# A planner's model of PSUM turns and of two operation costs, and the places of the keys' transfers and of the convolution's weights

## The chip, the cores and the metric

The kernel runs on one core of a Trainium2 chip. The metric is the device time of one execution in microseconds (us), smaller is better; a time given for a kernel is the median of several executions. Profiled executions carry a trace of every instruction, and their span is the time from the first to the last of them.

Engines are named as the profile names them: PE multiplies matrices, DVE and ACT work on vectors, POOL does small side work, and SP issues every transfer (DMA).

## What is computed

Two layers of a decoder trunk on 512 tokens of width 1024. Each layer projects its input to four branches, gates each branch, projects it back, merges the four and normalises. Cut to what matters here:

```python
for l in range(2):
    h = x @ W_in                      # one projection, its columns shared out to the branches
    ya = rwkv7(...)                   # 8 heads x 64: decay, delta-rule state over time
    yb = latent_attention(...)        # 8 heads, low-rank q and kv, one rotary key for all heads, causal
    yc = conv_module(...)             # glu -> causal depthwise conv, width 31 -> LayerNorm -> swish
    ym = cross_attention(x, mem, ...) # 4 heads x 128 over 256 memory tokens
    out = merge(gate(ya), gate(yb), gate(yc), gate(ym)) @ W_out
    x = LayerNorm(alpha * x + out)
```

Everything is float32. A product is made as three passes over a high and a low part of each factor (high by high, high by low, low by high), so each weight block of 128x1024 is loaded, rounded to its high part by ACT (names like `w11h`) and its rest taken by DVE (`w11l`).

## The kernel before

The program is written by a planner. `Plan` (L69) keeps a clock for PE, ACT, DVE and POOL, the time at which each tile was last written (`done`), and a queue of tasks, which are Python generators. Each task says up to which time it must wait, and the planner always lets the task run whose time is due by PE's clock; when none is due, the main stream goes on. What a task issues is put on the engines at that place and stays in that order, so the planner's guess of the times fixes the order on every engine, and the chip's semaphores then add the true waits. The guess has these parts:

- `Plan.start` (L91): an operation starts when its engine is free and each tile it reads or writes is done, plus a latency for the way from one engine to the other. Tiles that are only read hold nobody up.
- `Engine.__getattr__` (L210): the cost of an operation from its size. An ACT operation costs 65 + 0.83 ns per column, with more for a scale or a bias in a tile; the sum that it may leave beside (`accum_out`) costs nothing. A DVE reciprocal falls under the rule for all others, 65 + 1.04 ns per column.
- `Space` (L243): PSUM tiles, taken and given back; a tile that takes over a slot waits for the last use of the one before. The tags "ps" and "pp" are the PSUM tiles that the tasks share.

**Weights.** The main stream is a list of items; an item names the weight blocks that it needs, the work that it does with them, and a condition for being picked. The stream picks the next item whose condition holds, and asks for its weights ahead: up to four blocks (`LOOK`), through two raw buffers (`WR`) and three pairs of split buffers (`WH`). Every transfer stands in one queue, on SP, in program order, so a transfer that waits for its data holds up all behind it.

**The convolution** has four pairs of items (`conv_items`): glu0 to glu3 give the gate, val0 to val3 the value, each a projection of 24 passes. val of a pair may be picked when `L["glus"]` is above its number; this counter goes up when the gate's activation is issued, behind its 24 passes.

**The rotary key** (`key_rotary`): one 32x512 key for all heads is split into `krh` and `krl`, and these are copied by eight transfers into the eight tiles `kT` (four pairs, high and low), 2 us of the planner's time between pairs, starting when the split is done.

**RWKV units** (`rwkv_unit`): two units of four heads per half, eight in all (two layers). In each unit PE fills the tile `y0` (named `x_..x` in the trace): its left half is read by DVE into `BP` (two multiplies), its right half by ACT into `RA` (two copies), in this order, by the task `others`. After it, `w` is PE's small product of the running state `S`, and `QQ`, `PP` are DVE's steps of the next inverse.

**The softmax of the latent attention** runs per block of queries: PE makes scores `ms`, DVE masks them and takes the maximum (`nmm`), ACT takes the exponential with its row sum (`mP`, `smm`), DVE takes the reciprocal and scales, PE transposes `mP` into `mt`, ACT copies it (`mPT`), and PE makes `mo`. `xs`, `xP`, `xt`, `xo` are the same steps of cross-attention.

Nearly all instructions come from four helper lines: L237 (DVE, ACT, POOL), L288 (matmul), L293 (transpose) and L300 (transfer), so they are told apart by tile names.

Of the kernel before, what the change touches and what calls it, by code (L numbers as in the profile page):

```python
# [62 lines left out]
CH_P, CH_RG, CH_MG, CH_U, CH_CG, CH_XQ, CH_XG, CH_M = 0, 13, 17, 21, 29, 33, 37, 41  # L63
# [3 lines left out]
class Plan:  # L67
# [13 lines left out]
    def __init__(self, keep):  # L81
        self.keep = keep
        self.clk = {"PE": 0.0, "ACT": 0.0, "DVE": 0.0, "POOL": 0.0}
        self.t = self.queue = self.wires = 0.0
        self.cut, self.cuts = (128, 128), 0
        self.tasks = []
        self.done = {}
        self.seen = {}
        self.slots = {}

    def start(self, eng, outs, ins):  # L91
        s = self.clk.get(eng, 0.0)
        for n in outs + ins:
            t, e = self.done.get(n, (0.0, eng))
            s = max(s, t + self.lat(e, eng))
        return s

    def end(self, eng, t, outs, ins):
        for n in outs:
            self.done[n] = (t, eng)  # L100
        for n in outs + ins:
            self.seen[n] = max(t, self.seen.get(n, 0.0))

    def op(self, eng, cost, outs, ins):
        t = self.start(eng, outs, ins) + cost
        self.clk[eng] = t
        self.end(eng, t, outs, ins)
        self.t = max(self.t, t)
# [92 lines left out]
def _names(*aps):  # L201
    return [a.tensor.name for a in aps if hasattr(a, "tensor")]


class Engine:
# [5 lines left out]
    def __getattr__(self, name):  # L211
        f = getattr(self.eng, name)

        def call(*a, **k):
            o = k.get("out", a[0] if a else None)
            i = k.get("in_", k.get("in0", a[1] if len(a) > 1 else o))
            n = 1
            for d in (o if name in ("activation", "copy") or self.key == "POOL" else i).shape[1:]:
                n *= d
            if self.key == "ACT":  # L220
                c = 65 + 0.83 * n + 120 * hasattr(k.get("scale"), "tensor") + 90 * hasattr(k.get("bias"), "tensor")
            elif self.key == "POOL":
                c = 200 + 167 * n if k.get("op") == ALU.pow else 250 + 1.6 * n
            elif name == "tensor_tensor_scan":
                c = 65 + 2.1 * n
            elif name == "scalar_tensor_tensor":
                c = 128 + 1.04 * n if hasattr(k["scalar"], "tensor") else 75 + 1.03 * n
            elif name == "tensor_scalar" and hasattr(k["scalar1"], "tensor"):
                c = 152 + 1.12 * n if hasattr(k["scalar2"], "tensor") else 134 + 0.52 * n
            elif name in ("tensor_scalar", "tensor_copy"):  # L230
                c = 70 + 0.85 * n
            else:
                c = 65 + 1.04 * n
            args = list(a) + list(k.values())
            outs = _names(o, k.get("accum_out"))
            self.plan.op(self.key, c, outs, [x for x in _names(*args) if x not in outs])
            return self.plan.keep(f(*a, **k))  # L237

        return call


class Space:
# [18 lines left out]
    def tile(self, shape, dt, tag, name, bufs=None):  # L261
        t = self.pool.tile(shape, dt, tag=tag, name=name, **({} if bufs is None else {"bufs": bufs}))
        self.plan.slot((id(self.pool), tag), bufs or self.bufs, t.tensor.name)
        return t


@with_exitstack
def trunk_kernel(ctx: ExitStack, tc: tile.TileContext, A, out, dbg=None):
    nc = tc.nc
    plan = Plan(tc.keep_in_program_order)  # L270
    V, S, G = Engine(plan, nc.vector, "DVE"), Engine(plan, nc.scalar, "ACT"), Engine(plan, nc.gpsimd, "POOL")
# [30 lines left out]
    def pool(bufs, **k):  # L302
        return Space(plan, ctx.enter_context(tc.tile_pool(bufs=bufs, **k)), bufs)
# [7 lines left out]
    pp = pool(2, name="pp", space=PSUM)  # L311
# [29 lines left out]
    def cc(n):  # L341
        return cst[:, CCOL[n][0]:CCOL[n][1]]
# [297 lines left out]
    def layer_items(l):  # L640
        items = []
        L = {}
# [12 lines left out]
        def item(blocks, run, ready=None, picked=None, soon=None):  # L655
            items.append((blocks, run, ready, picked, soon))

        def ch_item(i, name, after, ready=None, picked=None):

            def run(get):  # L660
                ps = yield from project(get, X[l], name + t_)
                after(ps)
                yield
            item([(A["w_ch"][l, i], (512, 512))], run, ready, picked)
# [92 lines left out]
        SUB = range(2)  # L757
# [5 lines left out]
        def by2(ap):  # L763
            return ap.rearrange("p (a b) w -> p a b w", a=2)
# [5 lines left out]
        def rwkv_unit(j0, hf, rkv):  # L770
            t = f"_{l}_{j0}_{hf}"
# [8 lines left out]
            def rk(tag, shape, name=None, dt=F32, bufs=1):  # L780
                return L["rp"].tile([128] + shape, dt, tag=tag, name=(name or tag) + t, bufs=bufs)
# [27 lines left out]
            bt, kt, w = rk("bt", [2, 256]), rk("kt", [2, 256]), rk("s4", [2, 256], "w")  # L809
# [16 lines left out]
            for s in SUB:  # L826
                for cp, c2, h in quads:
                    c = 2 * cp + c2
                    MM(g0[HALF[c2], h, 128 * s + 64 * cp:128 * s + 64 * cp + 64], bt[HALF[h], s, 64 * c:64 * c + 64], AR[HALF[h], s, c, 0], start=True, stop=True, four=True)
            for s in SUB:  # L830
                for cp, c2, h in quads:
                    c = 2 * cp + c2
                    MM(g0[HALF[c2], h, 256 + 2 * s + cp:257 + 2 * s + cp], sq[HALF[h], s, 64 * c:64 * c + 64], bones2[HALF[h], h:h + 1], start=True, stop=True, four=True)
            gvs = [g1[:, :, 256 * s:256 * s + 256].rearrange("p h (a w) -> p h a w", a=2) for s in SUB]
            for s in SUB:
                for cp, c2, h in quads:
                    c = 2 * cp + c2
# [131 lines left out]
            x0, y0 = yield from pg.take([128, 2, 512], "x0" + t, 2, soon)  # L969
            x0, y0 = (x.rearrange("p c (q s a w) -> p q s c a w", q=2, s=2, a=2) for x in (x0, y0))  # L970
# [5 lines left out]
            for s in SUB:  # L976
                for cp, c2, h in quads:
                    c = 2 * cp + c2
# [10 lines left out]
            def others():  # L989

                yield
                for s in SUB:
                    V.tensor_tensor(out=by2(BP[s])[:, :, :, 64:128], in0=y0[:, 0, s],
                                    in1=cc("minc").unsqueeze(1).unsqueeze(1).to_broadcast([128, 2, 2, 64]), op=ALU.mult)
                for s in SUB:
                    S.copy(by2(RA[s])[:, :, :, 64:128], y0[:, 1, s].rearrange("p h c w -> p c h w"))
                pg.free()
                vt.extend((yield from tokens(2, vr, lambda: place("bt", "vt"))))

            vt = []  # L1000
            RA = [rk(f"s{4 + s}", [4, 128], f"RA{s}") for s in SUB]
# [53 lines left out]
            gb, hh, y0 = ([x[:, :, a:b].rearrange("p c (a w) -> p c a w", a=2) for x in gbs] for a, b in ((0, 256), (256, 384), (384, 512)))  # L1055
            for s in SUB:
                for cp, c2, h in quads:
                    MM(gb[s][HALF[h], c2, cp], VA[s][HALF[c2], 2 * (h ^ cp) + cp, 64:128], BP[s][HALF[c2], 2 * h + cp], start=True, stop=True, four=True)
                for cp in range(2):
                    for first in (True, False):  # L1060
                        for c2 in range(2):
                            for h in range(2):
                                e = 2 * h + cp
                                x, y = (bk1[s][:, e], vt[s][:, e]) if first else (BP[s][:, e, 0:64], VA[s][:, 2 * (h ^ cp) + cp, 0:64])
                                MM(hh[s][HALF[h], c2, cp], x[HALF[c2]], y[HALF[c2]], start=first, stop=not first, four=True)
                for h in range(2):
                    for first in (True, False):
                        for cp in range(2):
                            for c2 in range(2):
                                e = 2 * h + cp  # L1070
# [20 lines left out]
            for c in range(4):  # L1091
                e = 2 * (c % 2) + c // 2
                if hf == 0 and c == 0:
                    states.append([H[:, s, 0] for s in SUB])
                elif hf == 0 or c < 3:
                    ps, = yield from pa.take([128, 2, 64], f"w{c}" + t, 1, "pe" if diag else "small")
# [18 lines left out]
            ps, = yield from pg.take([128, 2, 512], "yb" + t, 1, soon)  # L1115
# [33 lines left out]
            ps, = yield from pa.take([128, 512], "ty" + t)  # L1149
# [101 lines left out]
        def conv_items(i):  # L1251
            d = {}

            def glu(ps):
                d["t"] = sp.tile([128, 512], F32, tag="tg", bufs=3, name=f"tglu{i}" + t_)
                S.activation(d["t"], ps, AF.Tanh, scale=0.5)
                L["glus"] += 1

            def val(ps):
                hpad = hpads[i % 2]  # L1260
                V.scalar_tensor_tensor(out=hpad[:, 30:542], in0=d["t"], scalar=1.0, in1=ps, op0=ALU.add, op1=ALU.mult)
                plan.spawn(taps(i, hpad))
                L["vals"] += 1

            ch_item(CH_U + 4 + i, f"glu{i}", glu, lambda: L["vals"] >= i - l and (i < 2 or L["taps"][i - 2] >= 20))
            ch_item(CH_U + i, f"val{i}", val, lambda: PRM[l] is not None and L["glus"] > i and (i < 2 or L["taps"][i - 2] == 30))


# [120 lines left out]
        def key_rotary():  # L1389

            kpe, ts = L["kpe"], u("rk" + t_, 256)
            k4 = kpe.rearrange("p (a d) -> p a d", a=4)
            yield lambda: angles
            rope(k4[:, :, 0:16], k4[:, :, 16:32], [ts[:, 64 * i:64 * i + 64].rearrange("p (a d) -> p a d", a=4) for i in range(4)], lambda f: f)
            ps, = yield from pa.take([128, 512], "kr" + t_)
            plan.due(kpe)
            yield "pe"
            for tb in range(4):
                TR(ps[0:32, 128 * tb:128 * tb + 128], kpe[:, 32 * tb:32 * tb + 32])
            yield  # L1400
            kr = [u(f"kr{n}" + t_, 512, F32R, 32) for n in "hl"]
            yield from split(*kr, ps[0:32])
            pa.free()
            plan.due(*kr)
            yield
            for kT in L["kT"]:
                for x, y in zip(kT, kr):
                    DMA(x[64:96].bitcast(F32), y.bitcast(F32))
                plan.t += 2000.0
                yield  # L1410
# [725 lines left out]
```

## Time and profile before

| what | value |
|---|---|
| time, median of 3 runs | 1481.37 us (1480.49 to 1482.63) |
| the profiled execution's own time | 1482.08 us |
| its span | 1480.3 us |
| granted PE clock, mean | 0.998 of full speed |
| PE busy | 1465.0 us, 99% of the span |
| DVE busy | 1037.4 us, 70% |
| ACT busy | 682.5 us, 46% |
| POOL busy | 145.2 us, 10% |

The rows of a timeline give an instruction's start in us, its length, engine, line, operation and tiles (output<-input); "x4" means a run of four like it, and a bracket tells how long the engine had been idle before it and what ended that. PE's passes overlap: the record of a pass lasts longer than the distance to the next one, so a gap between records is shorter than the time by which a pass started late.

### The profile page before, as it was taken

What the parts mean: (1) busy time and instruction counts of PE and PEld (TensorE: products, weight loads), DVE (VectorE), ACT (ScalarE), POOL (GpSimd) and SP (SyncE); (2) the same over time, 40 slices, a digit from 0 to 9 for tenths busy, and PEclk for the clock granted to TensorE, in tenths of its full rate; (3) what the DMA queues carried; (4) which work ended last, traced back from release to release, by engine and by line L of the source; (5) the groups of instructions that cost most, each with busy time, mean ns of one, the idle gap of its engine ahead of it and who ended that gap; (6) DMA issues with size and microseconds to landing.
All of it is one profiled execution on the core that took longest, in us unless ns stands there. A gap on an engine that the chain in (4) does not pass through costs nothing.

```text
span 1480.3 us, 28872 instructions
## 1 busy us (share of the span) xinstructions
PE 1465.0 (99%) x11727; PEld 1232.7 (83%) x11727; DVE 1037.4 (70%) x2022; ACT 682.5 (46%) x1327; POOL 145.2 (10%) x337
## 2 busy tenths in 40 slices
PE   9999999999999999999999999999999999999997
PEld 8888888888888888888999888888888788888886
DVE  6799998765757666545564889987856476756757
ACT  5546653425354544343264466633454454444331
POOL 0000000030303030000010000000041103121002
PEclk9999999999999999999999999999999999999999
DMA  6444332223232223333353252423232313233532
GB/s 216 139 127 110 86 115 93 93 75 97 68 89 74 84 75 103 122 117 130 113 165 109 74 148 74 121 92 104 81 95 76 95 51 106 71 101 113 172 94 78
DMA packets 89157, 153.49 MB, mean 104 GB/s; under 512 B 41024, under 2 KB 47424, under 8 KB 89024
## 3 DMA queue, kind: packets, MB, share of 16 engines
q1 hardware_dynamic: 89024, 151.65, 34.2%
q8 instruction: 92, 1.51, 0.4%
q14 instruction: 41, 0.34, 0.1%
HBM read 134.32 MB, written 5.77 MB: 95 GB/s over the span
## 4 chain that ended last, share of the span: by engine, by line
PE 89%; DVE 4%; DMA 3%; ACT 2%; POOL 1%; issue 1%; SPq 0%; ACTq 0%; DVEq 0%; POOLq 0%
PE ps_m L288 24%; PE po L288 12%; PE ps_cg L288 3%; PE ps_rg L288 3%; PE ps_xg L288 3%; PE ps_mg L288 3%; PE ps_xq L288 3%; PE ps_val L288 3%; PE ps_v L288 3%; PE ps_r L288 2%; PE pz L288 2%; PE ps_k L288 2%; PE ps_glu L288 2%; PE ms L288 2%; PE x L288 2%; DMA w<-in_w_ch_dram 1%
## 5 line engine op out<-in xcount | busy, mean ns | idle before, releaser
L237 DVE SCALAR_TENSOR_TENSOR cacc<-hpad,prm,cacc 128x512 f32<-128x512 f32 x240 | 179.1, 748 | 4.0
L237 ACT ACTIVATE tm<-ps_m,prm 128x512 f32<-128x512 f32 x64 | 44.1, 689 | 164.3 <-PE ps_m L288 163.6
L237 DVE SCALAR_TENSOR_TENSOR mt<-tm,po 128x512 f32<-128x512 f32 x48 | 33.0, 687 | 88.7 <-PE po L288 88.6
L237 POOL TENSOR_TENSOR tmpW<-ZT,W 64x14 f32<-64x14 f32 (+6 forms) x112 | 43.8, 391 | 8.0
L237 POOL TENSOR_SCALAR ZT<-W 64x256 f32<-64x256 f32 x8 | 5.8, 728 | 369.5 <-DMA W<-scr 144.6
L237 ACT ACTIVATE mP<-ms,nmm 128x128 f32<-128x128 f32 (+3 forms) x64 | 33.8, 530 | 17.6 <-DVE nmm L237 11.5
L237 POOL TENSOR_TENSOR ZT<-ZT,tmpW 64x14 f32<-64x14 f32 (+6 forms) x112 | 39.6, 354 | 8.8
L237 DVE TENSOR_TENSOR merged<-merged,mt 128x512 f32<-128x512 f32 x48 | 33.7, 702 | 1.7
L237 ACT COPY mPT<-mt 128x128 f32<-128x128 f32 (+3 forms) x64 | 26.1, 429 | 17.0 <-PE mt L293 16.6
L237 POOL MEMSET D<- 128x8 f32 x8 | 0.9, 112 | 327.0 <-PE ms L288 310.3
L237 DVE CUSTOM_DVE_ANT_0 ms<-ms,causal 128x128 f32<-128x128 f32 (+3 forms) x64 | 31.0, 499 | 0.2
L237 POOL TENSOR_SCALAR lrs<-lmv 128x1 f32<-128x1 f32 x8 | 4.0, 503 | 244.2 <-DVE lmv L237 239.3
L293 PE MATMUL mt<-cst,mP 128*128 128x128 f32 x160 | 26.3, 273 | 1.5 <-DVE smx L237 1.0
L237 DVE TENSOR_SCALAR mP<-mP,smm 128x128 f32<-128x128 f32 (+3 forms) x64 | 24.8, 387 | 2.4
L237 DVE SCALAR_TENSOR_TENSOR merged<-tm,po 128x512 f32<-128x512 f32 x16 | 11.0, 687 | 21.6 <-PE po L288 21.6
L293 PEld LDWEIGHTS mt<-cst,mP 128*128 128x128 f32 x160 | 19.6, 140 | 7.2 <-ACT xP L237 1.4
L237 ACT ACTIVATE yb<-yb,mr,gr 128x64 f32<-128x64 f32 x64 | 22.1, 428 | 2.9 <-DVE mr L237 2.9
L237 ACT ACTIVATE xP<-xs,nmx 128x256 f32<-128x256 f32 x32 | 15.2, 475 | 13.2 <-DVE nmx L237 11.4
L288 PE MATMUL ms<-kTl,qT 96*128 96x128 f32 (+3 forms) x64 | 21.1, 329 | 0.0
L237 ACT ACTIVATE z<-z,lnb,lrs 128x256 f32<-128x256 f32 (+2 forms) x11 | 7.0, 666 | 30.2 <-DVE lnb L237 30.2
L288 PE MATMUL ms<-kTh,qT 96*128 96x128 f32 (+3 forms) x64 | 20.6, 322 | 0.0
L288 PE MATMUL ms<-kTh,qTl 96*128 96x128 f32 (+3 forms) x64 | 20.6, 322 | 0.0
(3575 smaller groups left out, 5220.4 us busy)
## 6 DMA issues: line engine op xcount, KB each, us to landing
w<-in_w_ch_dram SPq DMA_DIRECT2D x146, 512.0 KB, 3.6
w<-in_w_o_dram SPq DMA_DIRECT2D x32, 512.0 KB, 3.6
w<-in_w_out_dram SPq DMA_DIRECT2D x16, 512.0 KB, 3.5
w<-in_w_lat_dram SPq DMA_DIRECT2D x15, 336.0 KB, 3.0
w<-in_w_mk_dram SPq DMA_DIRECT2D x8, 512.0 KB, 3.5
w<-in_w_mv_dram SPq DMA_DIRECT2D x8, 512.0 KB, 3.7
w<-in_w_qk_dram SPq DMA_DIRECT2D x8, 320.0 KB, 3.0
x<-in_xT_dram SPq DMA_DIRECT2D x8, 256.0 KB, 5.0
```

The costliest lines, as they stand in the source:

```text
L237: return self.plan.keep(f(*a, **k))
L288: plan.keep(nc.tensor.matmul(o, lhsT, rhs, start=start, stop=stop))
L293: plan.keep(nc.tensor.transpose(o, i, ident))
```

## The change

There are five edits, all in what the planner believes or in when a task asks for something. No operation of the computation is added or left out.

- **Turns.** PSUM tiles with the tags "ps" and "pp" now carry a note of who last read them and when. In the plan, an engine that reads such a tile starts no earlier than 130 ns after another engine's read has ended.
- **Costs.** An ACT operation that leaves a sum costs 130 ns more, and a DVE reciprocal costs 90 + 4 ns per column.
- **RA or BP first.** In `others`, ACT's copies into `RA` are issued ahead of DVE's multiplies into `BP` when ACT's clock stands behind DVE's.
- **Convolution weights.** In layer 0, `L["glus"]` goes up when glu is picked (`first`), not when its activation is issued, so val0's weights can be asked for right behind glu0's. In layer 1 it goes up as before.
- **Keys' transfers.** `key_rotary` waits 4 us of the planner's time before its first transfer.

```diff
@@ -87,12 +87,16 @@
         self.done = {}
         self.seen = {}
         self.slots = {}
+        self.read = {}
 
     def start(self, eng, outs, ins):
         s = self.clk.get(eng, 0.0)
         for n in outs + ins:
             t, e = self.done.get(n, (0.0, eng))
             s = max(s, t + self.lat(e, eng))
+        for n in ins:
+            t, e = self.read.get(n, (0.0, eng))
+            s = max(s, t + (130.0 if e != eng else 0.0))
         return s
 
     def end(self, eng, t, outs, ins):
@@ -100,6 +104,9 @@
             self.done[n] = (t, eng)
         for n in outs + ins:
             self.seen[n] = max(t, self.seen.get(n, 0.0))
+        for n in ins:
+            if n in self.read:
+                self.read[n] = t, eng
 
     def op(self, eng, cost, outs, ins):
         t = self.start(eng, outs, ins) + cost
@@ -218,9 +225,11 @@
             for d in (o if name in ("activation", "copy") or self.key == "POOL" else i).shape[1:]:
                 n *= d
             if self.key == "ACT":
-                c = 65 + 0.83 * n + 120 * hasattr(k.get("scale"), "tensor") + 90 * hasattr(k.get("bias"), "tensor")
+                c = 65 + 0.83 * n + 120 * hasattr(k.get("scale"), "tensor") + 90 * hasattr(k.get("bias"), "tensor") + 130 * ("accum_out" in k)
             elif self.key == "POOL":
                 c = 200 + 167 * n if k.get("op") == ALU.pow else 250 + 1.6 * n
+            elif name == "reciprocal":
+                c = 90 + 4 * n
             elif name == "tensor_tensor_scan":
                 c = 65 + 2.1 * n
             elif name == "scalar_tensor_tensor":
@@ -261,6 +270,8 @@
     def tile(self, shape, dt, tag, name, bufs=None):
         t = self.pool.tile(shape, dt, tag=tag, name=name, **({} if bufs is None else {"bufs": bufs}))
         self.plan.slot((id(self.pool), tag), bufs or self.bufs, t.tensor.name)
+        if tag in ("ps", "pp"):
+            self.plan.read[t.tensor.name] = 0.0, ""
         return t
 
 
@@ -989,11 +1000,19 @@
             def others():
 
                 yield
+
+                def right():
+                    for s in SUB:
+                        S.copy(by2(RA[s])[:, :, :, 64:128], y0[:, 1, s].rearrange("p h c w -> p c h w"))
+
+                first = plan.clk["ACT"] < plan.clk["DVE"]
+                if first:
+                    right()
                 for s in SUB:
                     V.tensor_tensor(out=by2(BP[s])[:, :, :, 64:128], in0=y0[:, 0, s],
                                     in1=cc("minc").unsqueeze(1).unsqueeze(1).to_broadcast([128, 2, 2, 64]), op=ALU.mult)
-                for s in SUB:
-                    S.copy(by2(RA[s])[:, :, :, 64:128], y0[:, 1, s].rearrange("p h c w -> p c h w"))
+                if not first:
+                    right()
                 pg.free()
                 vt.extend((yield from tokens(2, vr, lambda: place("bt", "vt"))))
 
@@ -1254,7 +1273,7 @@
             def glu(ps):
                 d["t"] = sp.tile([128, 512], F32, tag="tg", bufs=3, name=f"tglu{i}" + t_)
                 S.activation(d["t"], ps, AF.Tanh, scale=0.5)
-                L["glus"] += 1
+                L["glus"] += l
 
             def val(ps):
                 hpad = hpads[i % 2]
@@ -1262,7 +1281,11 @@
                 plan.spawn(taps(i, hpad))
                 L["vals"] += 1
 
-            ch_item(CH_U + 4 + i, f"glu{i}", glu, lambda: L["vals"] >= i - l and (i < 2 or L["taps"][i - 2] >= 20))
+            def first():
+                if l == 0:
+                    L["glus"] += 1
+
+            ch_item(CH_U + 4 + i, f"glu{i}", glu, lambda: L["vals"] >= i - l and (i < 2 or L["taps"][i - 2] >= 20), first)
             ch_item(CH_U + i, f"val{i}", val, lambda: PRM[l] is not None and L["glus"] > i and (i < 2 or L["taps"][i - 2] == 30))
 
 
@@ -1402,6 +1425,7 @@
             yield from split(*kr, ps[0:32])
             pa.free()
             plan.due(*kr)
+            plan.t += 4000.0
             yield
             for kT in L["kT"]:
                 for x, y in zip(kT, kr):
```

Since the order follows from the plan, it moves in many places. Three of them are shown; numbers behind a name are buffer numbers, and a bracket lists the queues whose semaphores a row waits for.

**SP, at the start of layer 0.** The rows are transfers; `in_w_ch` holds the projection's blocks, `in_w_mk` those of the memory's keys, `krh` and `krl` are the split rotary key. Before:

```order
L300 DMA w_464<-in_w_ch_dram 128x1024
L300 DMA w_494<-in_w_mk_dram 128x1024
L300 DMA w_537<-in_w_mk_dram 128x1024
L300 DMA kTh_0_356<-krh_580 32x512
L300 DMA kTl_0_357<-krl_581 32x512
L300 DMA w_609<-in_w_ch_dram 128x1024
L300 DMA kTh_0_358<-krh_580 32x512
L300 DMA kTl_0_359<-krl_581 32x512
L300 DMA kTh_0_360<-krh_580 32x512
L300 DMA kTl_0_361<-krl_581 32x512
L300 DMA w_648<-in_w_mk_dram 128x1024
L300 DMA kTh_0_362<-krh_580 32x512
```

After:

```order
L311 DMA w_464<-in_w_ch_dram 128x1024
L311 DMA w_494<-in_w_ch_dram 128x1024
L311 DMA w_537<-in_w_mk_dram 128x1024
L311 DMA w_603<-in_w_mk_dram 128x1024
L311 DMA kTh_0_356<-krh_583 32x512
L311 DMA kTl_0_357<-krl_584 32x512
L311 DMA w_649<-in_w_ch_dram 128x1024
L311 DMA kTh_0_358<-krh_583 32x512
L311 DMA kTl_0_359<-krl_584 32x512
L311 DMA kTh_0_360<-krh_583 32x512
L311 DMA kTl_0_361<-krl_584 32x512
L311 DMA w_699<-in_w_ch_dram 128x1024
```

val0's block, `w_609` before and `w_494` now, moves from behind the keys' first pair to the place right behind glu0's block (`w_464`); the two blocks of memory keys stay ahead of the pair, and what stands behind the pair now is the block of glu1, `w_649`.

**ACT and DVE, second unit of layer 1** (`x_1_0_1x` is its `y0`; `w194h` and `w194l` are the split of a weight block; `cb` is a PSUM tile of the convolution's output, which `yc` reads). ACT before, with its waits:

```order
L237 COPY PT_0_1_12808<-x_1_0_1_12734 128x4x64 x2
L237 COPY RA_1_0_1_12813<-x_1_0_1x 128x4x64 [waits DVE_49,PE_49]
L237 COPY RA_1_0_1_12814<-x_1_0_1x 128x4x64
L237 CAST w194h<-w_12878 128x1024 [waits DMAHW6_49,PE_49,Activation_49]
L237 ACTIVATE yc_1_12897<-cb_1_12880,prm_7759 128x512 [waits PE_49]
```

ACT after:

```order
L246 COPY PT_0_1_12808<-x_1_0_1_12734 128x4x64 x2
L246 COPY RA_1_0_1_12813<-x_1_0_1x 128x4x64 [waits PE_49]
L246 COPY RA_1_0_1_12814<-x_1_0_1x 128x4x64
L246 CAST w194h<-w_12878 128x1024 [waits DMAHW6_49,PE_49,Activation_49]
L246 ACTIVATE yc_1_12897<-cb_1_12880,prm_7759 128x512 [waits PE_49]
```

DVE before:

```order
L237 SCALAR_TENSOR_TENSOR mt_1_12824<-tm_1_12689,po_1_12724 128x512 [waits DVE_49,PE_49]
L237 TENSOR_TENSOR merged_1_10994<-merged_1_10994,mt_1_12824 128x512 [waits DVE_49]
L237 TENSOR_TENSOR BP_1_0_1_12510<-x_1_0_1x,cst 128x4x64
L237 TENSOR_TENSOR BP_1_0_1_12511<-x_1_0_1x,cst 128x4x64
L237 SCALAR_TENSOR_TENSOR S_1_0_0_12870<-w_1_0_0_12833,dl_0_0_11387,H_0_0_12216 128x64 [waits PE_49]
```

DVE after:

```order
L246 SCALAR_TENSOR_TENSOR mt_1_12824<-tm_1_12689,po_1_12724 128x512 [waits DVE_49,PE_49]
L246 TENSOR_TENSOR merged_1_10990<-merged_1_10990,mt_1_12824 128x512 [waits DVE_49]
L246 TENSOR_TENSOR BP_1_0_1_12510<-x_1_0_1x,cst 128x4x64 [waits Activation_49]
L246 TENSOR_TENSOR BP_1_0_1_12511<-x_1_0_1x,cst 128x4x64
L246 SCALAR_TENSOR_TENSOR S_1_0_0_12870<-w_1_0_0_12833,dl_0_0_11384,H_0_0_12216 128x64 [waits PE_49]
```

The rows keep their places; the wait between the two readers of `y0` changes sides. Of the eight units, ACT's `RA` waits for DVE in all eight before and in two after; in the other six DVE's `BP` waits for ACT.

**PE, softmax of layer 0** (the block whose transposed probabilities are made from `mP_0_1538` before and `mP_0_1539` after; their scores are `ms_0_1521` and `ms_0_1524`, a few rows earlier). Before:

```order
L288 MATMUL ms_0_1543<-kTl_0_363,qT_0_1208 128x128 [waits DMAHW6_49,DMAHW4_49,Activation_49]
L288 MATMUL ms_0_1543<-kTh_0_362,qT_0_1208 128x128 [waits DMAHW2_49]
L288 MATMUL ms_0_1543<-kTh_0_362,qTl_0_1209 128x128 [waits DMAHW0_49]
L293 MATMUL xt_0_1531<-cst,xP_0_1317 128x128 x2
L293 MATMUL xt_0_1531<-cst,xP_0_1421 128x128 x2
L293 MATMUL mt_0_1565<-cst,mP_0_1499 128x128 [waits DVE_49,Activation_49]
L293 MATMUL mt_0_1565<-cst,mP_0_1499 128x128 x3
L293 MATMUL mt_0_1573<-cst,mP_0_1538 128x128 [waits DVE_49,Activation_49]
L288 MATMUL ms_0_1575<-kTl_0_361,qT_0_1206 128x256 [waits Activation_49]
L288 MATMUL ms_0_1575<-kTh_0_360,qT_0_1206 128x256
L288 MATMUL ms_0_1575<-kTh_0_360,qTl_0_1207 128x256
```

After:

```order
L304 MATMUL mt_0_1557<-cst,mP_0_1501 128x128 [waits DVE_49,Activation_49]
L304 MATMUL mt_0_1557<-cst,mP_0_1501 128x128 x3
L299 MATMUL ms_0_1565<-kTl_0_361,qT_0_1206 128x256 [waits Activation_49]
L299 MATMUL ms_0_1565<-kTh_0_360,qT_0_1206 128x256
L299 MATMUL ms_0_1565<-kTh_0_360,qTl_0_1207 128x256
L304 MATMUL xt_0_1544<-cst,xP_0_1317 128x128 x2
L304 MATMUL xt_0_1544<-cst,xP_0_1424 128x128 x2
L299 MATMUL mo_0_1247<-mPT_0_1395,v_0_928 64x128 [waits Activation_49]
...
L299 MATMUL mo_0_1247<-mPT_0_1519,v_0_931 64x128
L304 MATMUL mt_0_1602<-cst,mP_0_1539 128x128 [waits DVE_49,PE_49]
L304 MATMUL mt_0_1610<-cst,mP_0_1552 128x128 [waits DVE_49,Activation_49]
```

The single transpose of that block stood behind four transposes of the block before; now three score passes, four transposes `xt` and the product `mo` stand between them.

## The prediction

> **What bounds the kernel now.** I read the page's busy shares and its chain first, then the busy time by stretches, then the list of what PE waited for, and last the timeline at each of those waits.
>
> ```profile
> PE 1465.0 (99%) x11727; PEld 1232.7 (83%) x11727; DVE 1037.4 (70%) x2022; ACT 682.5 (46%) x1327; POOL 145.2 (10%) x337
> PE 89%; DVE 4%; DMA 3%; ACT 2%; POOL 1%; issue 1%; SPq 0%; ACTq 0%; DVEq 0%; POOLq 0%
> ```
>
> PE is busy 1465.0 of 1480.3 us, and the chain that ended last runs through it. The edits take no pass away, so only two things can be won: time in which PE stands still, and the price of the order in which its passes stand. Where PE stands still:
>
> ```profile
> 100.00:150.00 50.00, 48.98 (x291) 41.29 (x290) 46.04 (x118) 31.72 (x81) 0.00 (x0) 1.00 0.52 133
> 150.00:200.00 50.00, 49.01 (x314) 40.97 (x313) 46.25 (x110) 30.28 (x74) 0.00 (x0) 1.00 0.37 102
> 900.00:950.00 50.00, 50.00 (x316) 42.15 (x315) 45.67 (x106) 31.24 (x73) 0.00 (x0) 1.00 0.47 123
> 1150.00:1200.00 50.00, 48.74 (x686) 40.25 (x685) 26.26 (x58) 25.26 (x54) 5.39 (x15) 1.00 0.25 72
> PE w L288 <- ACT yc L237: 1.3, 1, 1.3
> PE mt L293 <- DVE smx L237: 1.0, 1, 1.0
> PE mt L293 <- DVE mP L237: 0.5, 1, 0.5
> PE ps_val L288 <- DVE w11l L237: 0.5, 1, 0.5
> PE w L288 <- DVE S L237: 0.4, 1, 0.4
> PE ps_xq L288 <- ACT xql L237: 0.4, 1, 0.4
> ```
>
> The first numbers of a window row are its length and the busy times of PE, its weight loads, DVE and ACT. PE's clock is 1.00 in all of them, so a stall is worth its own length. Layer 0's softmax (100 to 200 us) loses 2.0 us on PE while DVE is busy 92% of it; layer 1's (900 on) loses nothing at nearly the same DVE load. So this is a matter of order, which is what the change moves. The rows behind the windows are what PE waited for, as gaps between records, and these are too short:
>
> ```profile
> 148.59 0.39 PE L288 MATMUL ps_xq<-xl,w29h 128*128 128x512 f32 x1
> 151.11 0.39 PE L288 MATMUL ps_xq<-xh,w29l 128*128 128x512 f32 x1
> 152.49 0.63 PE L293 MATMUL mt<-cst,mP 128*128 128x128 f32 x4 [0.99 <-DVE smx L237]
> 49.48 0.50 PE L288 MATMUL ps_val<-xh,w11l 128*128 128x512 f32 x1 [0.53 <-DVE w11l L237]
> 49.82 0.40 PE L288 MATMUL ps_val<-xl,w11h 128*128 128x512 f32 x1
> ```
>
> From the first ps_xq row to the second are 11 steps: 2.52 / 11 = 0.229 us a pass, 0.16 shorter than the record. The transposes at 152.49 should have begun at 151.34 and are 1.15 late, not 0.99: a stall is the gap plus 0.16. A 512-column pass behind a stall also keeps its successor 0.34 away (49.48 to 49.82) and not 0.229, which adds 0.11.
>
> **The change part by part.** First what it removes.
>
> *val0's weights.*
>
> ```profile
> 26.53 7.37 SPq L300 DMA_DIRECT2D w<-in_w_mk_dram  x2
> 41.37 0.63 SPq L300 DMA_DIRECT2D kTh<-krh  x1
> 42.71 0.53 SPq L300 DMA_DIRECT2D w<-in_w_ch_dram  x1
> 47.12 1.05 ACT L237 CAST w11h<-w 128x1024 fp32r<-128x1024 f32 x1 [2.11 <-DMA w<-in_w_ch_dram]
> 48.22 0.50 PE L288 MATMUL ps_val<-xl,w11h 128*128 128x512 f32 x1 [0.31 <-ACT w11h L237]
> L288 PE MATMUL ms<-kTl,qT x64: 223/338/481, 116.2 to 954.9; 96*128 96x128 f32 x16, 96*128 96x256 f32 x16, 96*128 96x384 f32 x16, 96*128 96x512 f32 x16
> ```
>
> SP issues nothing from 33.9 to 41.37, where the key's first pair waits for its split; val0's block stands behind that pair, lands at 47.1, and both halves of its split are what PE waits for. By the gaps: 0.31 + 0.16 + 0.11 and 0.53 + 0.16 + 0.11, together 1.38 us. Now the block is second in the queue, ahead of the empty stretch, and the one behind the pair is glu1's, which PE needs val0's 24 passes later: 24 x 0.229 = 5.5 us of cover against a delay that was 1.38. I take **-1.38**. The keys' transfers move back by 4 us of the plan and behind one block each (3.6 us to land by the page's row for such blocks, quoted below). What hides that is the distance to their reader, the scores ms, whose first pass stands at 116.2 us by the last row (range of starts): more than 60 us. In layer 1 PE works as long on other branches between the two. I cost it at **0**; without that cover it would be up to 4 us on the first ms.
>
> *Softmax of layer 0.*
>
> ```profile
> 133.43 0.30 PE L293 MATMUL mt<-cst,mP 128*128 128x128 f32 x1 [0.53 <-DVE mP L237]
> 134.38 2.40 PE L288 MATMUL mo<-mPT,v 128*64 128x128 f32 x40
> 145.27 0.50 PE L288 MATMUL ps_xq<-xl,w29h 128*128 128x512 f32 x1 [0.40 <-ACT xql L237]
> L237 ACT ACTIVATION_READ_ACCUMULATOR mP<-ms,nmm 128x1 f32 x64 | 12.8, 200 | 0.0
> ```
>
> The planner held the row sum that ACT reads out for free; it takes 0.2 us, so the plan believed mP ready too early. With its cost in, the single transpose at 133.43 (0.53 + 0.16 = 0.69 late) gets the 40 passes of mo, 2.3 us, ahead of it: **-0.69**. ps_xq at 145.27 (0.40 + 0.16 + 0.11 = 0.67 late, for a PSUM slot that ACT was still reading) now stands about 3 us of passes later: **-0.67**. The transposes at 152.49 (1.15 late) get four more transposes and three more ps_xq passes ahead, about 1.1 us of work: **-1.1**.
>
> *The two waits among the RWKV units.*
>
> ```profile
> 416.69 1.23 DVE L237 TENSOR_TENSOR w70l<-w,w70h 128x1024 fp32r<-128x1024 f32 x1 [3.92 <-ACT w70h L237]
> 418.16 0.52 PE L288 MATMUL w<-S,Gs 64*64 64x64 f32 x8 [0.43 <-DVE S L237]
> ACT RA L237 <- DVE BP L237: 13.9, 8, 3.7
> w<-in_w_o_dram SPq DMA_DIRECT2D x32, 512.0 KB, 3.6
> 1171.35 0.33 SPq L300 DMA_DIRECT2D w<-in_w_o_dram  x1
> 1176.09 0.65 ACT L237 COPY RA<-x_1x 128x256 f32<-128x256 f32 x2 [3.69 <-DVE BP L237]
> 1176.53 0.63 PE L293 MATMUL tk<-cst,v 128*128 128x128 f32 x4
> 1177.57 0.79 ACT L237 ACTIVATE yc<-cb,prm 128x512 f32<-128x512 f32 x1
> 1178.42 0.45 PE L288 MATMUL w<-S,Gs 64*64 64x64 f32 x8 [1.26 <-ACT yc L237]
> ```
>
> At 418 DVE makes S only after a weight's split; the stall is 0.43 + 0.19 (small passes overlap more) = 0.62. Six projection passes, 6 x 0.229 = 1.37 us, now stand ahead of w: **-0.62**. At 1178 ACT idles 3.69 us for BP, then does RA, a cast and yc, and w waits for the slot that yc gives back. With RA first, the cast starts when its block lands, 1171.35 + 3.6 = 1174.95, and ends at 1176.0; the transposes that yc reads are over by 1176.6, so yc starts at about 1176.7 in place of 1177.57: **-0.87** of the stall.
>
> The row at 1176.09 shows that a reader waits for a mere reader, though the other half of the tile is its own. [...]
>
> Not reached, as their order stands as it was: the start-up, four shorter waits, and the rest at 1178, 1.26 + 0.19 - 0.87 = 0.58.
>
> Sum of what goes: 1.38 + 0.69 + 0.67 + 1.1 + 0.62 + 0.87 = **5.33 us**.
>
> *What it adds.* PE's order now visits the 64x64 tile form 60 times, not 58. A visit:
>
> ```profile
> 1173.50 0.39 PE L288 MATMUL po<-ymg3h,w191l 128*128 128x512 f32 x1
> 1173.82 0.38 PE L288 MATMUL w<-S,Gs 64*64 64x64 f32 x5
> 1178.80 0.50 PE L288 MATMUL ps_m<-xl,w192h 128*128 128x512 f32 x1
> 1179.13 0.40 PE L288 MATMUL ps_m<-xh,w192h 128*128 128x512 f32 x1
> ```
>
> Going in costs 0.32 - 0.229 = 0.09. Going out: the eighth w starts 0.45 - 0.22 = 0.23 behind the first, at 1178.65, and ps_m follows 0.15 later where small passes follow each other by 0.03: 0.12. The pass behind that comes 0.33 - 0.229 = 0.10 late. Together 0.31, for two visits **+0.62**.
>
> *New waits.* About a third of the rows stand elsewhere, and the trace of before can't show a wait that isn't there yet. Lower bound nothing: layer 1's softmax runs 50 us without one. Upper bound 2.5: what layer 0's softmax, the place with the least slack, loses now by its three rows, 0.69 + 0.67 + 1.15. In the new order a few chains are shorter than any such chain was, mo behind its copied mPT above all (1.8 us of passes, at least 2.1 before). I take **+1.0**, nearer the lower end, because most such chains got longer.
>
> The turns themselves put no instruction and no wait into the program; what they cost is in these two terms. Net -5.33 + 0.62 + 1.0 = -3.71. The profiled execution took 1482.08 us (span 1480.3, 1.78 outside it), 0.71 above the median of the runs. 1482.08 - 3.71 = 1478.4 in a like execution, and less 0.71, **1477.7 us** for the median.
>
> **Rivals.**
>
> *The softmax takes its gain back.* DVE at 92% is the nearest second bound; a wait that passes moves behind the next DVE step. Then the 2.46 us of that part stay lost: 1477.7 + 2.5 = 1480.2. For it: both waits of mt there end with a DVE step. Against it: layer 1 at 91% loses nothing.
>
> *The weights' wait only moves.* The block behind the keys' pair still lands at 47.1. If PE reaches glu1 early, 1.38 comes back: 1479.1. Against it are the 5.5 us of cover. This is also the case in which the change doesn't do what it says.
>
> *Slower: DVE now waits for ACT.* Eight units show 13.9 us in which ACT idled for BP, free since ACT is 46% busy. Six units turn round, 13.9 x 6/8 = 10.4 us that can fall on DVE, in front of S, QQ and PP, for which PE waits in small passes. In the first of layer 0's second pair of units, ACT's gate reads from PSUM stand between its copies PT and RA, so BP waits for PE's projection too. If two thirds reach PE: +6.9, the two RWKV gains lost, +1.5: 1477.7 + 8.4 = 1486.1. It decides from about 5.2 us on PE, half of the 10.4: 1477.7 + 1.5 + 5.2 = 1484.4. Against it: DVE is 53% busy there, and ACT goes first only where the plan sees it ahead.
>
> **How the numbers follow.** Forecast 0.63, softmax gives back 0.19, the weights' wait moves 0.06, slower 0.12. A measurement of this kernel can tell about 0.2%, 2.96 us: faster is below 1478.4, slower above 1484.3. Of the forecast's 0.63, its own range 1475.0 to 1479.0, I put 0.60 below that line; with the rest same is 0.28 and slower 0.12. The range ends at 1474.5 below: no new waits (-1.0), the visits hidden (-0.62) and the rest at 1178 gone (-0.58) give 1475.5, and 1.0 goes to the spread of the runs, which reach 0.9 below and 1.3 above their median. It ends at 1482.5 above: the softmax gain lost and new waits at their upper bound, 1480.2 + 1.5 = 1481.7, and 0.8 of spread.
>
> **What would show it.** In the profile of the changed kernel: no PE wait at 45 to 55 us and the cast of val0's weights well before 42; PE above 49.6 of 50 in both windows between 100 and 200; no wait on S near 418; the wait on yc near 1178 at about 0.4; the idle time of RA for BP a few us in place of 13.9, and that of BP for RA below 2 us. The forecast is wrong if PE's waits between 100 and 200 stand at 2 us again, if layer 1's softmax, 900 to 1000, shows less than 49.5 of 50, or if DVE idles for RA by more than 5 us in all.

## The result, and the profile after

The changed kernel takes 1477.56 us (median of 10 runs, 1476.73 to 1478.02), the kernel before 1481.21 in the same comparison (10 runs, 1480.45 to 1482.63): a ratio of 0.9974, 95% interval 0.9965 to 0.9984. The forecast was 1477.7. The profiled execution after has a span of 1475.8 us, 4.5 shorter than before; the medians differ by 3.65, since the profiled execution of before was itself 0.87 above its median.

The page after (busy shares, and the chain that ended last), then what PE waited for, then the same windows as before:

```profile
PE 1464.4 (99%) x11727; PEld 1233.2 (84%) x11727; DVE 1037.1 (70%) x2022; ACT 681.0 (46%) x1327; POOL 144.5 (10%) x337
PE 96%; DVE 1%; ACT 1%; DMA 0%; POOL 0%; issue 0%; SPq 0%; POOLq 0%
```
```profile
PE warm L299 <- POOL reset L246: 1.3, 1, 1.3
PE pl L299 <- DVE w1l L246: 0.6, 1, 0.6
PE mt L304 <- ACT mPT L246: 0.4, 1, 0.4
PE w L299 <- ACT yc L246: 0.2, 1, 0.2
PE po L299 <- ACT tm L246: 0.2, 1, 0.2
```
```profile
100.00:150.00 50.00, 49.57 (x296) 41.90 (x295) 46.36 (x122) 33.63 (x87) 0.00 (x0) 1.00 0.53 131
150.00:200.00 50.00, 50.00 (x322) 42.55 (x321) 46.61 (x110) 29.56 (x73) 0.00 (x0) 1.00 0.36 101
900.00:950.00 50.00, 50.00 (x310) 42.05 (x309) 44.79 (x101) 27.57 (x64) 0.00 (x0) 1.00 0.46 126
1150.00:1200.00 50.00, 49.76 (x692) 41.05 (x691) 27.73 (x60) 28.12 (x59) 2.38 (x4) 1.00 0.26 72
```

The chain is now 96% PE in place of 89%. The waits of PE on val0's weights, on smx and mP, on xql and on S are gone, and that on yc is down from 1.3 to 0.2. Two are new: the transposes mt wait 0.4 for their PSUM slot, and po 0.2. DVE is as full between 100 and 200 as it was (93% after 92), yet PE stands still for 0.43 us in place of 2.0. Of the signs that the prediction named one is missed, by little: the window from 100 to 150 shows 49.57, not above 49.6, because of the new wait on mt. The others came: val0's weights are cast at 32.2, ACT idles 0.4 us for BP in place of 13.9, DVE 1.3 for RA, and layer 1's softmax stays at 50.00.

Where the time came from is read by laying the two traces side by side: the start of PE's first pass with a given weight block, before, after, and the difference.

| first pass with | before | after | difference |
|---|---|---|---|
| w8 (glu0) | 35.52 | 35.71 | +0.19 |
| w20 (memory values) | 89.25 | 87.92 | -1.32 |
| w28 (pq) | 141.20 | 138.60 | -2.60 |
| w34 (ps_xq) | 192.03 | 188.58 | -3.45 |
| w68 (ps_k) | 410.50 | 406.92 | -3.58 |
| w118 (end of layer 0) | 722.83 | 719.22 | -3.61 |
| w164 (behind layer 1's softmax) | 997.94 | 993.86 | -4.08 |
| w190 (ps_m) | 1160.36 | 1156.52 | -3.84 |
| w200 (ps_cg) | 1234.26 | 1229.41 | -4.85 |
| w220 (po, last) | 1373.28 | 1368.80 | -4.48 |

From w8 to w20, at val0, 1.5 us are won, in layer 0's softmax 2.1, over the RWKV units of layer 0 0.1, in layer 1 up to the end of its softmax 0.5 and at yc 1.0; some 0.6 is given back among the units of layer 1 (0.24 ahead of w190, 0.37 behind w200).

### The profile page after: what moved, and what is told of

The parts are those of the page before. It is cut to its first block, busy times and chain, and to the rows that moved or that the text cites. A ratio compares the mean times of both kernels' runs of the same rounds, so it can differ in the third digit from the quotient of the medians.

```text
span 1475.8 us, 28869 instructions
## 1 busy us (share of the span) xinstructions
PE 1464.4 (99%) x11727; PEld 1233.2 (84%) x11727; DVE 1037.1 (70%) x2022; ACT 681.0 (46%) x1327; POOL 144.5 (10%) x337
## 4 chain that ended last, share of the span: by engine, by line
PE 96%; DVE 1%; ACT 1%; DMA 0%; POOL 0%; issue 0%; SPq 0%; POOLq 0%
PE ps_m L299 24%; PE po L299 12%; PE ps_v L299 3%; PE ps_rg L299 3%; PE ps_cg L299 3%; PE ps_xg L299 3%; PE ps_xq L299 3%; PE ps_mg L299 3%; PE ps_k L299 3%; PE ps_val L299 3%; PE ps_glu L299 3%; PE ps_r L299 3%; PE pz L299 2%; PE ms L299 2%; PE pl L299 2%; PE x L299 2%
## 5 line engine op out<-in xcount | busy, mean ns | idle before, releaser
L246 POOL TENSOR_TENSOR tmpW<-ZT,W 64x14 f32<-64x14 f32 (+6 forms) x112 | 40.8, 365 | 8.0
```

## The experiments

Two theories stood against each other. A: each part of the change removes the wait that the prediction gave to it, and would do so alone. B: a part pays only in the order that the other parts leave to it. Times are medians; the kernel before had 1481.41 beside the first four, 1481.44 beside the next four and 1481.36 beside the last.

| kernel | time | against before, 95% interval |
|---|---|---|
| e1, RA edit alone | 1480.13 | 0.9982 to 1.0000 |
| e2, both transfer edits alone | 1480.10 | 0.9984 to 1.0002 |
| e3, costs alone | 1489.21 | 1.0037 to 1.0062 |
| e4, turns alone | 1487.20 | 1.0026 to 1.0053 |
| e5, all but RA | 1482.12 | 0.9991 to 1.0009 |
| e6, all but the transfer edits | 1488.63 | 1.0031 to 1.0056 |
| e7, all but costs | 1479.59 | 0.9977 to 0.9994 |
| e8, all but turns | 1480.22 | 0.9983 to 1.0001 |
| e9, RA and transfer edits | 1479.05 | 0.9974 to 0.9992 |
| e10, val0's weights alone | 1481.70 | 0.9992 to 1.0009 |
| e11, changed kernel, ACT 2 ns dearer | 1478.25 | 0.9970 to 0.9988 |
| e12, all but the keys' edit | 1486.12 | 1.0017 to 1.0040 |

**One part at a time (e1 to e4).** e1 has the hunk on `others`, e2 those on `conv_items` and `key_rotary`, e3 the two cost lines, e4 the notes of reads in `Plan` and `Space`, each as in the change and nothing else. One line of each, of the first cost line only its new end:

```diff
 e1:
+                first = plan.clk["ACT"] < plan.clk["DVE"]
 e2:
+                if l == 0:
+                    L["glus"] += 1
+            plan.t += 4000.0
 e3:
+ 130 * ("accum_out" in k)
+                c = 90 + 4 * n
 e4:
+            s = max(s, t + (130.0 if e != eng else 0.0))
```

> Only the edit that lets ACT's copies into RA go ahead of DVE's multiplies into BP. The order of instructions on each engine stays that of the kernel before; only the waits between the two readers turn round, in seven of the eight units. Theory A (each part of the change removes the wait that the prediction gave to it): 0.9 us less than before, 1480.3; PE's wait on yc near 1178 falls from 1.26 to about 0.4, ACT's idle time for BP from 13.9 us to about 2. Theory B (any new order shifts the time by an us or two, whatever it was meant for): no order moves, so no change, within 0.3 us of before.

> Only the two edits on transfers: val0's weights asked for with glu0's, the keys' transfers 4 us later in the plan. Theory A: 1.4 us less than before, 1479.8, with no PE wait on val0's weights and the waits in layer 0's softmax, near 418 and near 1178 where they were, 2.5 + 0.6 + 1.3 us. Theory B: the order moves in 200 of PE's rows, so the softmax's waits move too, and the sum is anywhere from 1479 to 1483.

> Only the planner's costs of ACT's sums and DVE's reciprocals. Theory A: the two waits of the transposes mt on DVE in layer 0's softmax go (0.69 + 1.15), val0's weights, ps_xq and the two RWKV waits stay: 1.8 less than before, 1479.4. Theory B: 750 of PE's rows move, the named waits may stay or go and others come; between 1479 and 1483 with no relation to the two waits.

> Only the turns of two readers of a PSUM tile in the plan. Theory A: ps_xq's wait for its PSUM slot (0.67) and w's wait near 418 (0.62) go, val0's weights and the waits of mt stay: 1.3 less than before, 1479.9. Theory B: 900 of PE's rows move; between 1479 and 1483, waits of mt gone or new at random.

e1 and e2 came out near A's 1480.3 and 1479.8, 1.3 us below before each; B's "no change" for e1 failed. Their intervals touch 1, so it is the trace that carries them. Rows of the timeline of e1, near 1176:

```profile
1172.05 0.69 ACT L237 COPY RA<-x_1x 128x256 f32<-128x256 f32 x2
1175.04 0.75 DVE L237 TENSOR_TENSOR BP<-x_1x,cst 128x256 f32<-128x256 f32 x2
1175.21 1.06 ACT L237 CAST w194h<-w 128x1024 fp32r<-128x1024 f32 x1 [2.47 <-DMA w<-in_w_o_dram]
1176.35 0.78 ACT L237 ACTIVATE yc<-cb,prm 128x512 f32<-128x512 f32 x1
1177.18 0.45 PE L288 MATMUL w<-S,Gs 64*64 64x64 f32 x8 [0.23 <-ACT yc L237]
```

RA is done 2.3 us before BP starts, the cast starts when its block lands, and w waits 0.23 in place of 1.26. In the four traces with the RA edit that were laid beside before (the changed kernel, e1, e9, e11) the passes behind this wait gain 0.99 to 1.03 us. The other waits of before are still there, but for the first and shorter of the two on val0's weights (0.31 us before).

e3 and e4 fell on the other side from A: 7.8 and 5.8 us slower, and beyond B's 1483 too. The longest waits of PE in e3 (the start-up's row left out), and rows of the timeline around the first of them:

```profile
PE ps_glu L290 <- DVE w149l L239: 2.3, 1, 2.3
PE mt L295 <- ACT xPTh L239: 2.0, 2, 1.3
PE w L290 <- ACT yc L239: 1.3, 1, 1.3
PE mt L295 <- DVE mP L239: 1.0, 1, 1.0
```
```profile
887.64 1.07 ACT L239 CAST w149h<-w 128x1024 fp32r<-128x1024 f32 x1
888.59 1.07 ACT L239 CAST w150h<-w 128x1024 fp32r<-128x1024 f32 x1
890.21 0.61 ACT L239 ACTIVATE txg<-ps_xg 128x512 f32<-128x512 f32 x1
890.86 0.69 DVE L239 SCALAR_TENSOR_TENSOR xg<-txg,ps_xg 128x512 f32<-128x512 f32 x1 [1.59 <-ACT txg L239]
891.46 1.22 DVE L239 TENSOR_TENSOR w149l<-w,w149h 128x1024 fp32r<-128x1024 f32 x1
892.73 0.50 PE L290 MATMUL ps_glu<-xh,w149l 128*128 128x512 f32 x1 [2.33 <-DVE w149l L239]
```

The plan put both casts next to each other ahead of txg on ACT, and xg ahead of w149l on DVE: DVE idles 1.59 us for txg with the split that PE needs queued behind. It is not the transfer: the block was asked for at 875.0, and such blocks land 3.6 us later in the median of before. In the changed kernel it is asked for at 871.2, and w149l stands well ahead of xg (it starts at 878.1). e4 has a like one at the end, po waiting 2.3 us for yrg2l, and 1.8 for w11l. The waits in the trace of e3 don't tell the whole of its median: its profiled execution, at 1486.4, is the fastest of five, and the other four take 1488.4 to 1489.6 at a lower mean clock (0.996 or 0.997 for 0.998); the last section has a likely reason.

**One part out (e5 to e8).**

> The changed kernel without the edit on RA and BP. Theory A (this part is worth its wait wherever the rest of the order goes): 1.3 us above the changed kernel, as it was 1.3 below before by itself: 1478.9, with PE's wait on yc near 1175 back at 1.3. Theory B (parts pay only in the order that they meet): the plan moves in 170 of PE's rows, so anything from 1477 to 1482.

> The changed kernel without the two edits on transfers. Theory A: 1.3 to 1.4 us above the changed kernel, 1478.9, with two waits on val0's weights near 48. Theory B: with turns alone the waits on val0's weights grew to 2.4 us in place of 1.2 and halved PE's clock behind them; that comes back, and the time is 1481 or more.

> The changed kernel without the planner's costs of sums and reciprocals. Theory A (each part alone is worth its waits): the waits of mt in layer 0's softmax come back, 1.8 us: 1479.4. Theory B (costs and turns each make the plan wrong in another place, and only both together set it right): costs alone were 7.8 slower than before, turns alone 5.8, so a wait of 1.5 us or more stands somewhere, and the time is above 1481.

> The changed kernel without the turns on PSUM tiles. Theory A: ps_xq's wait and w's near 418 come back, 1.3 us: 1478.9. Theory B: as without the costs, a wait of 1.5 us or more in the softmax of either layer, and the time above 1481.

A is near in e7 alone (1479.4 expected). Without RA the kernel is 4.6 us above the changed one, without the transfer edits 11.1, where A had 1.3 and 1.4. B's range for e5 ended at 1482, just below the 1482.12, and its 1481 or more for e6 came true. The long waits of PE in e5 and in e6:

```profile
PE po L299 <- DVE yrg2l L246: 2.3, 1, 2.3
PE tk L304 <- ACT yc L246: 0.8, 1, 0.8
```
```profile
PE ps_glu L299 <- DVE w149l L246: 2.3, 1, 2.3
PE xt L304 <- DVE xP L246: 1.7, 1, 1.7
PE ps_val L299 <- DVE w11l L246: 1.1, 1, 1.1
PE mt L304 <- DVE mP L246: 0.8, 1, 0.8
```

The long waits of e3 and e4 are back. The reason that B gave for e6 is the smaller part of it: w11l is waited for 1.1 us and w149l 2.3, in a profiled execution with a mean clock of 0.998. For e5, DVE's rows show part of how yrg2l comes late:

```profile
1371.94 1.22 DVE L246 TENSOR_TENSOR w222l<-w,w222h 128x1024 fp32r<-128x1024 f32 x1 [0.90 <-ACT w222h L246]
1373.08 0.68 DVE L246 TENSOR_TENSOR yrg2l<-r,yrg2h 128x512 fp32r<-128x512 f32 x1
```

It stands behind the split of a block that PE needs later (w222), for whose cast DVE idles 0.90 us. In the changed kernel it stands ahead of that split, at 1366.5.

In e7 and e8 B missed: no single wait of 1.5 us, and times of 1479.6 and 1480.2, below its 1481. But both keep the waits of layer 0's softmax, each of them both those on DVE steps and the one on xql (e7: smx 1.0, mP 0.6, xql 0.4; e8: mP 2.3 in three, xql 0.4). Beside the RA and the transfer edits, neither costs nor turns take these out alone; together they do, and e5 shows that they don't need the RA edit for it.

**Pairs, halves and a blind (e9 to e12).** e9 has the hunks of e1 and e2; e10 only the hunk on `conv_items`; e12 the changed kernel without the line on `plan.t`; e11 the changed kernel with

```diff
-                c = 65 + 0.83 * n + 120 * hasattr(k.get("scale"), "tensor")
+                c = 67 + 0.83 * n + 120 * hasattr(k.get("scale"), "tensor")
```

> The RA edit and the two transfer edits, without costs and turns; the order is that of the transfer edits alone, only the waits of the two readers of y0 turn round. Theory A (these parts add): 1.3 + 1.3 = 2.6 us below before, 1478.8, with the softmax waits of layer 0 (0.75, 0.56, 1.15) and w's near 416 (0.63) still there, so costs and turns together are worth the last 1.2. Theory B (parts pay only in the order that they meet): 1480.1, as each alone.

> Only val0's weights asked for with glu0's; the keys' transfers stay as before. Theory A: this edit alone takes the waits on val0's weights away, as val0's block goes ahead of the keys' first pair, 1.3 us below before: 1480.1. Rival: the second block of memory keys now stands behind the pair in the queue and PE waits for it in place of val0's, 1 us or more, so nothing is won without the keys' edit: 1481.4.

> The changed kernel with 2 ns more on every ACT operation in the plan (67 in place of 65), which no row of the trace asks for; 130 of PE's rows and 150 of DVE's and ACT's move. Theory A (the changed plan is nearer the chip, so a small error does it no harm): 1477.6, within 0.7. Theory B (its order is one lucky order among many): 1479 to 1483, with a wait of 1 us or more that the changed kernel hasn't got.

> The changed kernel without the 4 us ahead of the keys' transfers. Theory A (val0's weights do the work, the keys' edit only keeps the pair out of the way): 1477.6 to 1478.5. Rival: a block of memory keys stands behind the pair and is waited for, or the softmax loses its order as without both transfer edits (1488.6): 1481 or more.

e9 is 2.3 below before, where A had 2.6 and B 1.3: the two add, near enough. Its profiled execution has a longer wait on S near 416, 1.2 for 0.4, because the block whose split DVE does first landed later. Its cast in e2, and in e9:

```profile
413.39 1.05 ACT L237 CAST w70h<-w 128x1024 fp32r<-128x1024 f32 x1 [0.45 <-DMA w<-in_w_ch_dram]
```
```profile
414.02 1.05 ACT L237 CAST w70h<-w 128x1024 fp32r<-128x1024 f32 x1 [1.28 <-DMA w<-in_w_ch_dram]
```

The transfer was asked for at 409.46 and 409.38. In the fourteen traces it lands 3.9 to 4.6 us after that, latest in e9, so this wait hangs on 0.7 us of scatter in a transfer's time.

e10 wins nothing, so A missed, and the rival has the number but not the cause. The waits on val0's weights are gone, and the second memory block behind the pair costs 0.2 (hpad, for which PE waits, stands on DVE behind that block's split), not the 1 us of the rival; but layer 0's softmax moved, and mt now waits 1.4 and 0.7 us for mP and smm, with the clock at 0.50 behind them, from 134 to 137 us.

In e12 A missed by 8 us and the rival's 1481 or more came true. Its long waits, without the start-up's:

```profile
PE ps_glu L299 <- DVE w149l L246: 2.3, 1, 2.3
PE mt L304 <- DVE mP L246: 2.3, 3, 1.0
PE ps_glu L299 <- DVE w12l L246: 0.5, 1, 0.5
PE ps_xq L299 <- ACT xql L246: 0.4, 1, 0.4
```

Without the keys' edit the wait on w149l is back, and so are those of layer 0's softmax, as in e8; and PE waits for glu1's block (w12), which is asked for behind all four pairs of keys.

e11, in which 130 of PE's rows move where the costs alone move 750, is 0.7 above the changed kernel, at the edge of A's range, and has no wait above 0.4 but the start-up's: one such shift, at least, doesn't destroy the changed order.

Over all twelve, two patterns hold without an exception. w149l is waited for in the three kernels that have the costs and not the keys' edit (e3, e6, e12), and in no other. yrg2l is waited for in the two that have the turns and not the RA edit (e4, e5), and in no other. So two of the edits repair an order that two others would spoil. The rows above show, for yrg2l in part, which order is spoilt; how the keys' edit and the RA edit lead the plan to the better one was not followed.

## Why the prediction was right

**val0's weights**: -1.38 forecast, 1.5 measured from w8 to w20. Behind glu0 the block is split before SP's empty stretch, and glu1's isn't waited for, as its 5.5 us of cover had it (its split is done at 49.9, and PE asks for it at 54.15). The keys' edit was costed at 0 for its readers, and ms never waited for it in the changed kernel. What else it does was not seen: by e12 the changed kernel is 8.6 us slower without it.

**Softmax of layer 0**: -2.46 forecast for the three waits, less a share of the +1.0 for new ones. All three went, and one of 0.43 + 0.16 us came, mt behind the copy mPT that gives its PSUM slot back; the prediction had named the chain through that copy as shortened, though at its other end, mo. From w20 to w34 2.1 us were won. The size was right and the cause was not: the prediction gave the waits on mP and smx to the row sum that the planner had held for free. With that cost alone (e3) waits in these places stay and grow, and without it (e7) one sees the old ones; it takes costs, turns and the keys' edit together (e7, e8, e12).

**The two RWKV waits**: the wait on S near 418 is gone, -0.62, but over layer 0's units the difference only goes from -3.51 (at w54) to -3.61. A new wait on tm near 444 (0.19 + 0.16 + 0.11 = 0.46) and one of the two added visits to the small tile form (0.31 by the prediction's rows) ate it; these were in the sum as new waits and visits. yc: -0.87 forecast, -1.0 measured from w190 to w200, and e1 shows it to be the RA edit's own work.

**New waits and visits**, +1.62: 0.6 at mt, 0.46 at po, 0.31 for the visit in layer 0, and 0.6 given back in layer 1's units, where the other visit lies, 2.0 together. Two of the four shorter waits that were held to stay went as well, at 103.8 in layer 0 and 868 in layer 1, 0.36 and 0.39 with their restarts; the slow start of the first block cost 0.19.

**The sum.** The terms were about the right size, but the close agreement of the median, 0.1 us, is luck in part. By the pair of traces the differences add to -4.5, where -3.71 was forecast; by the medians it is -3.65. Between them stands the profiled execution of before, 0.87 above its median. Some of that is at val0: e1, whose order there is that of before, lacks the first of its two waits and is 0.4 us shorter from w8 to w12. So val0's term, read from one execution, was taken on the large side; where the rest of the 0.87 lies is open.

**The slower rival** named something that does occur, but small. What DVE waited for ACT's reading of y0 in the changed kernel, from the list of waits:

```profile
DVE BP L246 <- ACT RA L246: 1.3, 2, 0.7
```

1.3 us, where up to 10.4 could have fallen on DVE. In the six units in which ACT goes first DVE waits in two, 0.65 and 0.69 us, and in the other four RA is done before DVE comes; no wait of PE on BP is in the list. That the softmax takes its gain back, the first rival, happened in e10 and e12, not here.

**A step that was too short**: a stall was held to be worth its own length, read from windows in which the longest was 1.3 us. e5 and e12 show that it need not be for 2.4 (the clock behind it stood at 0.50 from 1374 to 1377 us in e5 and at 0.67 from 893 to 896 in e12), e4 for 1.9 (0.50), and e10 for two short ones in a row (0.50).

## What to carry to other kernels

A list scheduler's costs are not improved one by one: here the two that were to bring the plan nearer to the chip cost 6 to 8 us alone and win only beside the others, so test such edits together and look for the one or two long waits that each brings. A wait between two engines that merely read one tile could be turned round here (ACT idled 13.9 us for BP before, DVE 1.3 for RA after), and should lie on the engine that has nothing urgent behind it. A stall of PE of some 2 us, or two shorter ones close together, deserves attention first, for it may cost more than its own length: in e5 the clock stood at 0.50 for 3.2 us behind a stall of 2.4, and with passes of 0.43 us in place of 0.229 that is, by estimate, 1.5 us more.

## What the runs showed of the hardware

In these runs PE's granted clock stood at 0.50 behind some stalls of 1.9 to 2.4 us, and at 1.00 behind others (a stall is the gap between records plus 0.16, as in the prediction). Timeline of e5, where po waits for yrg2l, and the windows around (the granted clock is the third column from the end of a row):

```profile
1373.82 0.79 PE L299 MATMUL po<-yrg2l,w220h 128*128 128x512 f32 x1 [2.27 <-DVE yrg2l L246]
1374.84 0.63 PE L299 MATMUL po<-yrg2h,w220l 128*128 128x512 f32 x1
1375.27 0.63 PE L299 MATMUL po<-yrg3l,w220h 128*128 128x512 f32 x1
```
```profile
1370.00:1374.00 4.00, 1.73 (x8) 1.12 (x7) 3.10 (x5) 2.66 (x4) 0.00 (x0) 0.96 0.90 283
1374.00:1377.00 3.00, 3.00 (x8) 2.32 (x9) 0.58 (x2) 0.00 (x0) 0.00 (x0) 0.50 0.93 280
```

A pass takes 0.43 us there in place of 0.229, for 3.2 us after the stall, at a clock of 0.50. Behind the same wait on w149l the passes took 0.43 us in e12 too, and the clock was 0.67 from 893 to 896; in the profiled execution of e3 it stayed 1.00, and that of e6 has a mean clock of 0.998. In e12, and in e3:

```profile
893.00:896.00 3.00, 3.00 (x14) 2.42 (x13) 2.64 (x12) 0.70 (x3) 0.00 (x0) 0.67 0.85 227
```
```profile
893.00:896.00 3.00, 3.00 (x19) 2.40 (x19) 2.89 (x11) 0.83 (x4) 0.00 (x0) 1.00 0.58 154
```

e5's eleven runs fall into two groups near 2 us apart: five between 1480.1 and 1481.3 with a mean clock of 0.998 or 0.999, and six, the profiled one among them, between 1482.1 and 1483.0 at 0.997 (one at 0.998). The profiled executions of e3 and e6 are the fastest of their five, at 0.998, and the others, 2 to 4 us slower, have 0.996 or 0.997, so it looks as if they paid this too, but no trace shows it.

Shorter stalls show the same, and as irregularly. In e10 the clock stood at 0.50 from 134 to 137 us, behind two of 1.5 and 0.85 us within 3 us; around two of the same lengths near 136 in e4 it stayed 1.00. So it did around a single one of 1.9 near 170 in e6 (1.00 from 168 to 174); behind one of 1.9 near 50 in e4, 2.5 us after one of 0.3, it was 0.50. Windows of e4, behind the one near 50 and over the two near 136:

```profile
50.70:54.10 3.40, 3.40 (x12) 2.69 (x10) 1.88 (x2) 1.39 (x2) 0.00 (x0) 0.50 0.52 154
135.00:141.00 6.00, 5.20 (x57) 4.58 (x58) 5.77 (x18) 3.12 (x10) 0.00 (x0) 1.00 0.01 3
```

The stretch at 0.50 lasted 3.2 us in e5 and at least 3.4 in e4. What decides when the clock falls and for how long, no run shows.
